# A gated product over 32 row tiles: the first tile's store as two transfers of one row each

## The chip, the cores and the metric

The kernel runs on one core of one Trainium2 chip. The metric is the device time of one execution in microseconds (us). The kernel before takes 933.05 us, the median of three runs (932.90 to 933.36).

On a core, VectorE (DVE), ScalarE (ACT) and GpSimd (POOL) compute here; SyncE (SP) only issues transfers. Transfers issued by SP stand in one queue (q1 in the profile), those issued by ACT in another (q10), and both queues are served by the same 16 DMA engines.

## The reference

The input x is 8192 x 8192 in float32. Its left half a and its right half b make the output, 8192 x 4096:

```python
def reference(x: np.ndarray) -> np.ndarray:
    a, b = np.split(x, 2, axis=-1)
    return a * (1 / (1 + np.exp(-b)))
```

So 268.4 MB are read and 134.2 MB are written, and each output element needs one sigmoid and one multiply.

## The kernel before

The 8192 rows are cut into 32 tiles of 256 rows. In a tile each of the 128 partitions holds two whole neighbouring rows (R = 2): 64 KB of input and 32 KB of output per partition, each one contiguous piece of device memory. There are two input buffers and two output buffers (SLOTS = 2), and tile i uses number i % 2 of each.

`trace` (L120) writes the order out by hand. Load 0 is put ahead of everything else (`_launch_early`, L152), then comes load 1 (L124). Then for every tile i: the work, load i+2 and store i.

- **Load** (`load`, L49): one transfer of the whole tile, 8 MB, issued by SP at L51. From load 2 on, it waits until the product of tile i-2 is done, because that work reads the buffer it overwrites.
- **Work of tiles 1 to 30** (`work_shared`, L79): ACT makes the sigmoid in place for columns 0 to 767 of both rows (L90), then for the other 3328 columns of both rows (L93). POOL multiplies the first part (L96); DVE multiplies the second (L100). POOL waits on the semaphore `ready` of the slot. That semaphore counts two things: the first sigmoid of this tile, and the landing of the store that last read this output buffer, which is store i-2. DVE waits on `both`, which counts the second sigmoid and POOL's product. DVE's product raises `product`.
- **Work of tiles 0 and 31** (`work`, L56): four pieces of half a row, 2048 columns each, with sigmoids on ACT (L64) and products on DVE (L76). The first piece's product waits on `ready` too.
- **Store of tiles 0 to 30** (`store`, L106): one transfer of 4 MB issued by ACT at L110, when the tile's last product is done. ACT works in order, so the next tile's sigmoids come behind this issue and its wait. When a store lands it adds 16 to `ready`; the planner keeps in `stored` how much the next tile in this slot has to wait for:

```python
self.to_ready[s] += 1 + self.stored[s]
self.stored[s] = 0
```

- **Store of tile 31**: four transfers of 1 MB (8 KB per partition), issued by SP as the pieces get done.

Of the kernel before, what the change touches and what calls it, by code (L numbers as in the profile page):

```python
# [13 lines left out]
class _Program:  # L14
# [105 lines left out]
    def trace(self):  # L120

        n, half = self.n_tiles, self.half
        fourths = [(slice(r, r + 1), slice(h * half // 2, (h + 1) * half // 2)) for r in range(R) for h in range(2)]
        self.load(1)  # L124
        for i in range(n):
            if i in (0, n - 1):
                self.work(i, fourths)
            else:
                self.work_shared(i)
            if i + SLOTS < n:  # L130
                self.load(i + SLOTS)
            if i < n - 1:
                self.store(i)
        for k in range(4):
            self.store(n - 1, k * half // 2, (k + 1) * half // 2, self.products - 3 + k)
# [74 lines left out]
```

## Time and profile before

| | |
|---|---|
| median of 3 runs | 933.05 us |
| the profiled execution | 933.04 us |
| its span, first to last instruction | 931.7 us |
| bytes moved, mean rate over the span | 402.67 MB, 432 GB/s |
| DVE, ACT and POOL busy | 230.6, 229.6 and 103.3 us |
| a load, issue to landing (median of 32) | 43.7 us |
| a store from ACT, issue to landing (median of 31) | 36.3 us |
| the first store, issue to landing | 33.5 us |
| ACT waits for loads at L90 | 650.0 us in 30 waits |
| POOL waits at L96, all put down to ACT's L90 | 787.3 us in 30 waits |

The page begins with the busy time of the engines, then shows the span in 40 slices. Of its DMA queues it lists packets, megabytes and the time that the packets took, as a share of 16 engines over the span. A packet is what one DMA engine moves in one piece: a row of a transfer, that is 64 KB for a load and 32 KB for a store here, or a completion of a few bytes, of which each transfer has 16. The DMA view can be asked for a stretch of time; it then counts the packets that began in that stretch. The timeline lists instructions in order: start, duration, engine, line, what is written and read, and in brackets the idle time before it and what ended it. The chain of waits is followed back from the last instruction.

### The profile page before, as it was taken

What the parts mean: (1) busy time and instruction counts of PE and PEld (TensorE: products, weight loads), DVE (VectorE), ACT (ScalarE), POOL (GpSimd) and SP (SyncE); (2) the same over time, 40 slices, a digit from 0 to 9 for tenths busy, and PEclk for the clock granted to TensorE, in tenths of its full rate; (3) what the DMA queues carried; (4) which work ended last, traced back from release to release, by engine and by line L of the source; (5) the groups of instructions that cost most, each with busy time, mean ns of one, the idle gap of its engine ahead of it and who ended that gap; (6) DMA issues with size and microseconds to landing.
All of it is one profiled execution on the core that took longest, in us unless ns stands there. A gap on an engine that the chain in (4) does not pass through costs nothing.

```text
span 931.7 us, 252 instructions
## 1 busy us (share of the span) xinstructions
DVE 230.6 (25%) x38; ACT 229.6 (25%) x69; POOL 103.3 (11%) x34
## 2 busy tenths in 40 slices
DVE  0333202332023330233302333113331133311333
ACT  1323330233311333113331133311333113332033
POOL 0011110111100111001110011110111101111010
DMA  9999999999999999999999999999999999999999
GB/s 405 428 450 428 426 452 405 450 428 428 450 422 433 428 439 439 428 428 459 439 408 430 443 454 428 412 460 411 450 428 425 453 407 449 428 428 450 425 430 405
DMA packets 9649, 402.67 MB, mean 432 GB/s; under 512 B 1072, under 2 KB 1072, under 8 KB 1072
## 3 DMA queue, kind: packets, MB, share of 16 engines
q1 hardware_dynamic: 5184, 272.63, 67.7%
q10 hardware_dynamic: 4464, 130.03, 32.3%
q14 instruction: 1, 0.01, 0.0%
HBM read 268.44 MB, written 134.22 MB: 432 GB/s over the span
## 4 chain that ended last, share of the span: by engine, by line
DMA 75%; DVE 12%; ACT 12%; DVEq 0%; issue 0%
DMA x_sb<-in_x_dram 75%; DVE o_sb L100 11%; ACT x_sb L93 9%; ACT x_sb L90 2%; DVE o_sb L76 1%; DVEq L142 0%; ACT x_sb L64 0%
## 5 line engine op out<-in xcount | busy, mean ns | idle before, releaser
L100 DVE TENSOR_TENSOR o_sb<-x_sb 128x6656 f32<-128x6656 f32 x30 | 212.8, 7092 | 654.5 <-ACT x_sb L93 654.5
L90 ACT ACTIVATE x_sb<-x_sb 128x1536 f32<-128x1536 f32 x30 | 44.5, 1482 | 650.0 <-DMA x_sb<-in_x_dram 650.0
L96 POOL TENSOR_TENSOR o_sb<-x_sb 128x1536 f32<-128x1536 f32 x30 | 103.1, 3436 | 787.3 <-ACT x_sb L90 787.3
L93 ACT ACTIVATE x_sb<-x_sb 128x6656 f32<-128x6656 f32 x30 | 172.0, 5733 | 0.0
L76 DVE TENSOR_TENSOR o_sb<-x_sb 128x2048 f32<-128x2048 f32 x8 | 17.8, 2287 | 40.4 <-ACT x_sb L64 40.4
L64 ACT ACTIVATE x_sb<-x_sb 128x2048 f32<-128x2048 f32 x8 | 14.6, 1897 | 41.0 <-DMA x_sb<-in_x_dram 41.0
L64 ACT ACT_TABLE_LOAD x1 | 1.3, 1283 | 1.4 <-PEq L176 1.4
L194 POOL MEMSET const-float32-0.0<- 128x1 f32 x1 | 0.1, 98 | 0.2 <-issue 0.2
L194 POOL MEMSET const-bfloat16-1.0<- 128x1 bf16 x1 | 0.1, 101 | 0.0
L194 POOL MEMSET const-uint8-127<- 128x1 uint8 x1 | 0.1, 101 | 0.0
L194 POOL MEMSET const-float32-1.0<- 128x1 f32 x1 | 0.1, 98 | 0.0
## 6 DMA issues: line engine op xcount, KB each, us to landing
out_dram<-o_sb ACTq DMA_DIRECT2D x31, 4096.0 KB, 36.3
out_dram<-o_sb SPq DMA_DIRECT2D x4, 1024.0 KB, 5.8
x_sb<-in_x_dram SPq DMA_DIRECT2D x32, 43.7
```

The lines of the kernel that those rows point to most:

```text
L64: sig = nc.scalar.activation(out=b, in_=b, func=mybir.ActivationFunctionType.Sigmoid)
L76: mul = nc.vector.tensor_mul(out=packed[:, r, c], in0=rows[:, r, 0, c], in1=rows[:, r, 1, c])
L90: sig = nc.scalar.activation(out=rows[:, :, 1, c0], in_=rows[:, :, 1, c0], func=sigmoid)
L93: nc.scalar.activation(out=rows[:, :, 1, c1], in_=rows[:, :, 1, c1], func=sigmoid).then_inc(self.both[s], 1)
L96: mul = nc.gpsimd.tensor_mul(out=packed[:, :, c0], in0=rows[:, :, 0, c0], in1=rows[:, :, 1, c0])
L100: mul = nc.vector.tensor_mul(out=packed[:, :, c1], in0=rows[:, :, 0, c1], in1=rows[:, :, 1, c1])
L194: nc = _bacc.Bacc("TRN2", target_bir_lowering=False, num_devices=1)
```

## The change

The first tile's store, one transfer of 128 partitions x 32 KB, becomes two transfers of 128 partitions x 16 KB. The first moves row 0 of each partition (`store(0, 0, half)`), the second row 1 (`store(0, half)`). Both are issued by ACT one behind the other, and both wait for the product of the whole tile, as the one transfer did. Each adds 16 to `ready` of slot 0 when it lands, so POOL's product of tile 2 waits for both. All other tiles are as before.

```diff
             if i + SLOTS < n:
                 self.load(i + SLOTS)
-            if i < n - 1:
+            if i == 0:
+                self.store(0, 0, half)
+                self.store(0, half)
+            elif i < n - 1:
                 self.store(i)
         for k in range(4):
             self.store(n - 1, k * half // 2, (k + 1) * half // 2, self.products - 3 + k)
```

## The prediction, made before the result was known

> **What bounds the kernel now.** I read the page first: its parts 2 to 4 say what is busy and what ended last.
>
> ```profile
> DMA  9999999999999999999999999999999999999999
> ...
> q1 hardware_dynamic: 5184, 272.63, 67.7%
> q10 hardware_dynamic: 4464, 130.03, 32.3%
> ...
> DMA 75%; DVE 12%; ACT 12%; DVEq 0%; issue 0%
> ```
>
> The two queues' packets take 67.7 + 32.3 = 100.0% of the 16 DMA engines' span, while the busiest compute engine has 25%. So the chain's 24% of DVE and ACT cannot be cut out of the time: transfers run beside them. The DMA view cut to short stretches shows how the engines divide themselves. First 4 to 33 us, loads alone; then 46 to 60.5 us, a load beside the first store; then 38.7 to 42.3 us, one round.
>
> ```profile
> DMA packets 208, 12.58 MB, mean 434 GB/s; under 512 B 16, under 2 KB 16, under 8 KB 16
> ```
>
> ```profile
> DMA packets 128, 6.29 MB, mean 434 GB/s; under 512 B 0, under 2 KB 0, under 8 KB 0
> ...
> q1 hardware_dynamic: 64, 4.19, 66.7%
> q10 hardware_dynamic: 64, 2.10, 33.5%
> ```
>
> ```profile
> q1 hardware_dynamic: 16, 1.05, 67.2%
> q10 hardware_dynamic: 16, 0.52, 33.7%
> ```
>
> Loads alone: 208 - 16 completions = 192 packets of 64 KB, 12 for each engine in 29 us, so a load row takes 29/12 = 2.417 us. Mixed: 4 packets from each queue per engine in 14.5 us, so a round is 3.625 us and a store row of 32 KB takes 1.208. The rate is 434 GB/s both ways, and **each queue gets one packet a turn, whatever its size**: equal counts, bytes 2 to 1. The timeline dates the first tiles.
>
> ```profile
> 32.82 0.38 ACTq L110 DMA_DIRECT2D out_dram<-o_sb  x1
> 44.76 1.48 ACT L90 ACTIVATE x_sb<-x_sb 128x1536 f32<-128x1536 f32 x1 [15.49 <-DMA x_sb<-in_x_dram]
> ...
> 51.91 7.09 DVE L100 TENSOR_TENSOR o_sb<-x_sb 128x6656 f32<-128x6656 f32 x1 [19.12 <-ACT x_sb L93]
> 59.03 0.36 ACTq L110 DMA_DIRECT2D out_dram<-o_sb  x1
> 73.72 1.48 ACT L90 ACTIVATE x_sb<-x_sb 128x1536 f32<-128x1536 f32 x1 [21.84 <-DMA x_sb<-in_x_dram]
> ```
>
> Tile 1 is done 14.3 us after it lands (44.76 to 59.03); tiles follow each other every 29 us, which is 8 rounds of 3.625. The end is read from the DMA view of 921.6 to 930.2 us:
>
> ```profile
> DMA packets 496, 3.67 MB, mean 427 GB/s; under 512 B 48, under 2 KB 48, under 8 KB 48
> ```
>
> The four last stores still run at full rate after the last multiply (925.5). Their 448 data packets of 8 KB are 28 per engine in 8.6 us, 0.307 each. A count of all packets gives the span: 256 load rows x 2.417 + 248 store rows x 1.208 + 32 x 0.307 = 618.7 + 299.6 + 9.8 = 928.1, plus 1.0 before the first, plus about 0.7 for the first and 0.8 for one slow load row as the first store joins (16 packets at 34 to 38.7 us took 69.1% of 4.7 us, 3.25 each): 930.6 of 931.7 us. Nothing but packets is in it.
>
> **The change part by part.** Only the first store changes. *Bytes and packets*: 8 rows of 32 KB per engine become 16 of 16 KB. No 16 KB row is in the trace; from below it is half a 32 KB row, 0.604, from above two 8 KB rows, 0.614. Sixteen cost 9.66 to 9.82 against 8 x 1.208 = 9.66: **+0.0 to +0.2 us**, and I take 0.604, as the rate is 434 from 32 KB up and 427 at 8 KB. A gain is excluded, since no stretch passes 434. One more completion is 0.01 us.
>
> *Issue*: a second DMA on ACT right behind the first, its wait already met, 0.38 us by the first's row. Behind it is tile 1's sigmoid, not due before 43.5, so it costs nothing; without that cover it would cost 0.38.
>
> *Turns*: a store row is half as big, so beside a load the round is 2.417 + 0.604 = 3.021, not 3.625: **loads go faster, the first store slower**. I check the count on the kernel before. Store packets start at 38.7 (in 34 to 38.7 only q1 has any). A completion counts as a turn: store 0's 8 rows lie between 7 load rows and load 1's completion, 38.7 + 8 x 1.208 + 7 x 2.417 = 65.3, and it lands at 66.3 (32.82 + 33.5 of the DMA view), 1.0 later. Load 2: 9 load rows (the last of load 1, eight own) and 10 store rows, 38.7 + 21.75 + 12.08 = 72.5; tile 2 starts at 73.72, 1.2 later. Now with halves:
>
> - Load 1 lands after one load row and two halves: 38.7 + 2.42 + 1.21 + 1.2 = 43.5, 1.2 earlier; tile 1 is done at 57.8.
> - Load 2: 38.7 + 21.75 + 10 x 0.604 + 1.2 = 67.7, 6.0 earlier.
> - Store 0: 16 halves and the first half's completion are 17 turns against 15 load rows and two completions: 38.7 + 9.66 + 36.26 = 84.6, landing at 85.6 instead of 66.3.
>
> *A new wait*: tile 2 writes the buffer that store 0 reads, and POOL's multiply (L96) waits for it. Its sigmoid is there at 69.2, the store at 85.6, so **POOL waits 16 us**, ends at 89.1, and DVE (L100) runs from 89.2 to 96.3. Without the wait DVE would have ended at 82.0; before, it was 88.0. Behind DVE's product hang load 4 on SP and store 2 on ACT, and behind store 2 on ACT tile 3's sigmoids. Does the DMA run dry? At 84.6 load 3 has 2 rows left: 84.6 + 2 x 2.417 + 2 x 1.208 = 91.9, and then the load queue is empty. Store 1, issued at 57.8, has 6 rows left, alone: 7.25 us, to 99.1. Load 4 and store 2 are issued at 96.3. From issue to first packet I have the first of the last stores: issued at 918.94, and packets of its queue begin at 920.9, 2.0 us. So they are ready at 98.3, **0.8 us before the engines run dry**. What hides the whole stall is this backlog of store 1; each microsecond beyond 0.8 is paid in full. A load that joins may cost one slow row as at 35 us, +0.8, or nothing as when the last stores joined; I take nothing, the nearer in kind (a queue used before).
>
> *Afterwards*: load 4 has 8 load rows and 7 store rows, 99.1 + 19.3 + 8.5 + 1.2 = 128.1, where before it was 131.7, so a lead of 3.6 us stays. Store 1 lands at 102.6, POOL of tile 3 waits for it, DVE ends at 113.3; load 5 is in the queue well before 127. Store 2 lands at 131.6, tile 4's POOL ends at 135.1, and its second sigmoid at 135.2: the wait is covered. Then each tile repeats in 29 us, 3.6 us early. At the end the last load lands 3.6 earlier, at 911.1, but that much more of the stores is still to move: the bytes are the same, the engines never idle, and the last packet comes when it did. **Sum: +0.0**, between +0.0 and +1.0 (packets 0.2, slow row 0.8).
>
> The profiled execution took 933.04 us, 1.3 more than its span, and the median is 933.05, so the forecast is 933.04 + 0.06 = **933.1 us**.
>
> **The rivals.**
> - *The shares do not move* (a turn is a fixed amount of bytes, not a packet), and the change shows nothing of the above: 933.0. Against it: a completion of 4 bytes takes a turn in the counts above. 10%.
> - *The engines run dry* (slower): tile 2's stall outlasts store 1's backlog at 99.1 us. It decides from 2.8 us between issue and first packet. For it: the first store was issued at 32.8 and its packets began at 38.7, 5.9 us. Then load 4 and store 2 begin at 102.2, 3.1 us late, all of it lost: 936.1. Against it: that was ACT's first transfer, behind load rows of 2.4 us each; and the last stores needed 2.0. 10%.
> - *The second transfer's start is not overlapped*: 2.0 us from issue to first packet as idle engines, 935.1. Against it: the three later last stores follow one another at 427 GB/s. 3%. The Trainium skill's page "DMA: Bandwidth & Descriptors", section "Anatomy of one DMA — SWDGE (gpsimd) path", puts a fixed cost of about 2.0 us on every DMA beside its bytes, and would add that much here; the 427 GB/s over the end of this trace speaks against adding it up.
> - *The end follows the last load* (faster): the chain of waits goes back from the last multiply to loads, and these come 3.6 us early: 929.4. Against it: after the last multiply 5 us of packets are left at full rate. 3%.
>
> **How the numbers follow.** My forecast has 74%. About 0.2% (1.9 us) is what a measurement here can tell from no change. Forecast and unmoved shares are within it: same 84%; dry engines and start cost: slower 13%; faster 3%. Range: below, the slow row of 35 us could vanish, 933.1 - 0.8 = 932.3; above, the sum's +1.0 and the start cost's 935.1. So 932.3 to 935.1, leaving out the rest of the dry case and the faster case, some 12%.
>
> **What would show it.** The DMA view at 46 to 57 us should have equal packet counts and bytes 4 to 1. Tile 1's first sigmoid should start at 43.5, tile 2's at 67.7, with POOL's wait of 16 us put down to the store; DVE of tile 2 should end at 96.3; load 4 should land at 128.1, the later ones 3.6 us early; and no stretch between 85 and 105 us should be below 420 GB/s. I am wrong if tile 2 is done after 97.1 or a load issued into an empty queue needs more than 2.8 us.

## The result, and the profile after

| | before | changed |
|---|---|---|
| median of 22 runs each | 933.26 us | 936.57 us |
| lowest and highest | 932.90 to 934.14 | 932.93 to 963.15 |
| the profiled execution, its span | 933.04, 931.7 | 938.78, 937.5 |

The changed kernel is slower by 0.3%: the ratio is 1.0029 with an interval of 1.0016 to 1.0042. The two longest of its runs, 951.99 and 963.15 us, count as slow runs and are left out of the ratio, though their granted clock is 1.0 like that of the others. The forecast was 933.1 us, 932.3 to 935.1, so it was wrong.

The kernel before is steady; the changed one is not. Of its 22 runs 7 took 932.9 to 933.6 us, the forecast's time; 9 took 936.3 to 937.2, 4 took 938.0 to 942.2, and 2 took 952 and 963. So the question is what differs from run to run.

The page of the changed kernel, with the same lines as the page of before:

```profile
DMA  9999999999999999999999999999999999999997
...
q1 hardware_dynamic: 5184, 272.63, 67.4%
q10 hardware_dynamic: 4608, 130.03, 32.2%
...
DMA 75%; DVE 12%; ACT 11%; POOL 0%; DVEq 0%; issue 0%
```

Only the last digit of the DMA row has changed, from 9 to 7, and the two queues sum to 99.6% of a longer span. So the engines are as full as before until the very end. The store queue has 144 packets more: 128 more rows, because 128 rows of 32 KB became 256 of 16 KB, and 16 completions more.

The timeline of the changed kernel follows the forecast for the first 98 us. Columns: start, duration, engine and line, then the idle time before and what ended it.

```profile
43.27 1.48 ACT L90 ACTIVATE x_sb<-x_sb 128x1536 f32<-128x1536 f32 x1 [13.97 <-DMA x_sb<-in_x_dram]
...
57.55 0.36 ACTq L110 DMA_DIRECT2D out_dram<-o_sb  x1
67.47 1.48 ACT L90 ACTIVATE x_sb<-x_sb 128x1536 f32<-128x1536 f32 x1 [17.08 <-DMA x_sb<-in_x_dram]
...
85.57 3.42 POOL L96 TENSOR_TENSOR o_sb<-x_sb 128x1536 f32<-128x1536 f32 x1 [37.30 <-DMA out_dram<-o_sb]
89.02 7.09 DVE L100 TENSOR_TENSOR o_sb<-x_sb 128x6656 f32<-128x6656 f32 x1 [31.50 <-POOL o_sb L96]
96.14 0.36 ACTq L110 DMA_DIRECT2D out_dram<-o_sb  x1
...
113.14 0.36 ACTq L110 DMA_DIRECT2D out_dram<-o_sb  x1
...
129.10 1.48 ACT L90 ACTIVATE x_sb<-x_sb 128x1536 f32<-128x1536 f32 x1 [25.43 <-DMA x_sb<-in_x_dram]
```

Tile 1 lands at 43.27 (forecast 43.5), tile 2 at 67.47 (67.7). POOL's product of tile 2 starts at 85.57 (85.6); its sigmoid was there at 67.47 + 1.48 = 68.95, so it waited 16.6 us for the store. Load 4 and store 2 are issued at 96.14 (96.3). The large stall is there, as foreseen. In the list of waits, POOL's wait for a store now stands first, with 25 of its 30 tiles; this one is the longest:

```profile
POOL o_sb L96 <- DMA out_dram<-o_sb: 643.7, 25, 37.3
```

The 37.3 us are all of POOL's idle time before it, of which 16.6 us lie behind the sigmoid.

From 129 us on the forecast and the trace part. The last load should have landed at 911.1, 3.6 us earlier than before (914.68); it landed later:

```profile
916.79 7.31 ACT L64 ACTIVATE x_sb<-x_sb 128x2048 f32<-128x2048 f32 x4 [22.36 <-DMA x_sb<-in_x_dram]
```

The stretches at the end tell how. The last two columns are the share of time in which the 16 DMA engines moved packets, and GB/s. First the changed kernel, then the kernel before:

```profile
926.00:932.00 6.00, 1.63 (x1) 0.00 (x0) 0.00 (x0) 1.00 0.99 412
932.00:937.40 5.40, 0.00 (x0) 0.00 (x0) 0.00 (x0) 1.00 0.09 38
```

```profile
926.00:931.70 5.70, 0.00 (x0) 0.00 (x0) 0.00 (x0) 1.00 0.84 356
```

Up to 932 us the engines are full. From there on the share is 0.09, and 0.09 x 16 is 1.4 engines: one or two of the sixteen still work, for 5 us, while the others are done. The packets of each engine can be followed, since each begins where the one before on its engine ends. Fourteen engines end between 931.9 and 932.4 us, one at 934.7, one at 937.1. Before, all sixteen ended between 930.7 and 931.4. **Two engines of sixteen are late, and the transfer is done when the last engine is.**

They are not late from the start. Every load ends with one completion on each engine; this table, worked out from the packet records of the changed kernel, has for some loads the median time of the sixteen, the deviation of the two latest, and that of the other fourteen:

```
load's completion     the two engines      the other fourteen
128.4 us              -0.88   -0.88        -0.11 to 0.33
476.4                  0.47    1.75        -0.15 to 0.28
650.7                  1.90    2.52        -0.18 to 0.24
766.7                  2.07    3.13        -0.27 to 0.40
882.8                  2.18    4.17        -0.29 to 0.58
```

They begin 0.88 us ahead and slip by 3.1 and 5.1 us over 26 tiles. (In the first row the two stand apart as the earliest; between 130 and 420 us they pass through the others and can't be told from them by time alone.)

What sets these two apart happened when load 4 joined. The packets of the two kinds of engine there (S and L a row of a store and of a load, s a completion of store 1, each with its start):

```
fourteen engines: S 98.06   s 99.27   L 99.28    S 101.69   L 102.90
two engines:      S 98.50   L 99.70   s 102.12   L 102.12   S 104.54
```

The DMA view of the changed kernel in two short stretches shows it in counts of packets and MB. From 99.2 to 99.8 us:

```profile
DMA packets 30, 1.05 MB, mean 1748 GB/s; under 512 B 14, under 2 KB 14, under 8 KB 14
...
q1 hardware_dynamic: 16, 1.05, 403.9%
```

and from 102.11 to 102.14 us:

```profile
DMA packets 4, 0.13 MB, mean 4369 GB/s; under 512 B 2, under 2 KB 2, under 8 KB 2
...
q1 hardware_dynamic: 2, 0.13, 1007.5%
```

In the first stretch all sixteen begin load 4's first row, but only 14 small packets, store 1's completions, go with them. The two missing ones come 2.4 us later, each with a second load row right behind. On fourteen engines the store's completion comes **ahead of row 0** of the load, on two it comes **behind row 0**. Since every queue then goes on by turns, an engine keeps that order, tile after tile, to the end.

### The profile page after: what moved, and what is told of

Its sections match the earlier page's. It is cut to its first block, busy times and chain, and to the rows that moved or that the text cites. A ratio compares the mean times of both kernels' runs of the same rounds, so it can differ in the third digit from the quotient of the medians.

```text
span 937.5 us, 253 instructions
## 1 busy us (share of the span) xinstructions
DVE 230.6 (25%) x38; ACT 229.6 (24%) x69; POOL 103.2 (11%) x34
## 4 chain that ended last, share of the span: by engine, by line
DMA 75%; DVE 12%; ACT 11%; POOL 0%; DVEq 0%; issue 0%
DMA x_sb<-in_x_dram 70%; DVE o_sb L100 11%; ACT x_sb L93 8%; DMA out_dram<-o_sb 5%; ACT x_sb L90 2%; DVE o_sb L76 1%; POOL o_sb L96 0%; DVEq L145 0%; ACT x_sb L64 0%
```

## The experiments

Seventeen kernels were run, one of them twice. Their expectations speak of theories by letters. A, B and C are rivals from the start: A is the order of turns at the moment when load 4 joins, B the stall and POOL's wait for stores, C a fixed cost of a second transfer; e1 has them in full. G (the compute engines slow the load rows) and H (the order of loads and stores does so alone) are in full at e13. The other letters are explained where they come up.

For reading the runs it helps to have their common measure first. In the profile of each run the packets of every engine were followed from 100 to 880 us, and noted, for every load on every engine: behind which of its eight rows a store's completion comes, and how much longer than 8 x 2.418 us its rows took. "Ahead" means ahead of row 0.

```
kernel                 completion behind   loads x engines   extra us per load
before                 row 5               418               0.001
changed                ahead / row 0       339 / 52          0.001 / 0.170
e1_late                ahead               368               0.116
e2_early               ahead / row 0       335 / 26          0.001 / 0.202
e5_early_again         row 0 / ahead       250 / 144         0.662 / 0.759
e16_after_dve          row 1 / row 0       250 / 128         0.005 / 0.301
e3_parts               row 6               386               0.001
e9_first_half          row 5               357               0.001
e4_tiny1               row 4 / row 5       234 / 147         0.001 / 0.000
e6_dry_split           row 4 / row 5       246 / 124         0.000 / 0.004
e7_dry_clean           row 4 / row 5       254 / 145         0.001 / 0.000
e8_one                 row 5 / row 4       412 / 18          0.001 / 0.006
e18_shift_less         row 5               406               0.001
e10_shift              row 0               404               0.603
e11_shift_one          row 0 / row 7       368 / 20          0.547 / 0.504
e12_shift_eight        row 0 / row 7       241 / 130         0.560 / 0.126
e13_shift_nowork       row 0               397               0.563
e14_shift_dve          row 0 / row 1       361 / 28          0.589 / 0.445
e15_shift_noact        row 0               396               0.586
```

All lines but the first two are of runs told below; e17 turned out to be e10 again and has no line. Entries of fewer than 18 loads are left out. Wherever completions come behind row 0 for load after load, the loads are slow; with them behind rows 4 to 6 they are slow in none of these runs. Behind other rows, or ahead, they are free in some runs, and slow in e5, e11, e12 and e14, where more than half of the engines stand behind row 0, and in e1.

### The halves by themselves

**Only the first half is stored.** Row 1 of each partition of tile 0 is left out of the output.

```diff
-            if i < n - 1:
+            if i == 0:
+                self.store(0, 0, half)
+            elif i < n - 1:
                 self.store(i)
```

> The kernel before, but of the first store only the first transfer of the change is made: row 0 of each partition, 8 packets of 16 KB per engine. Row 1 of the first tile (half its output) is left out, so 2.1 MB less are written: 8 x 0.604 = 4.8 us less for each engine. Eight packets are eight turns, as many as the whole store has in the kernel before, so that tile 2 does not wait, the load queue does not run empty and the loads are not ahead. Theory A: 928.0 to 929.5 in nearly every run, with no slow rows. Rival D (half rows of 16 KB themselves cost, or put the engines out of step): above 930.

Measured: 928.19 us, median of 5 runs, ratio 0.9952 (0.9938 to 0.9965). The 2.1 MB left out are 8 rows of 16 KB per engine, 8 x 0.604 = 4.8 us, and 933.26 - 4.8 = 928.4. So rows of 16 KB move at their price. There is only one transfer here, so this says nothing of the start of a second one.

**Two transfers cut by partitions instead of by rows**, in the kernel before:

```diff
-            if i < n - 1:
+            if i == 0:
+                self.store(0, parts=slice(0, 64))
+                self.store(0, parts=slice(64, P))
+            elif i < n - 1:
                 self.store(i)
```

> The first store goes as two transfers, but each of 64 partitions with whole 32 KB rows, not of half rows. Each engine then has the 8 packets of 32 KB of the kernel before and one completion more. Theory A: store 0 lands at most one load row (2.4 us) later, tile 2 does not wait for it, the load queue never runs empty, all engines stay in step: 933.0 to 933.6. Theory B: no stall, 933.0 to 933.6. Theory C (fixed cost of a second transfer): 935 to 936.5.

Measured: 937.19 us, median of 5, ratio 1.0034 (1.0021 to 1.0047). The kernel before had 934.04 us beside it, so this is outside what any of the three theories gave. It was no clean control, since it has a loss of its own and at once: between 54 and 68 us, in the second of the two transfers, most rows of 32 KB took 1.3 to 1.8 us instead of 1.21, and after 75 us no row is slow. In the first of the two most rows took 1.21 us, and some 1.3 to 1.44. The Trainium skill's page "SBUF — State Buffer", section "Door 1: The DMA port swizzle (why `[64,N]` ≈ `[32,N]`)", says that 64 partitions in a row reach no more ports than 32 do; the second transfer's rows fit that and most of the first's do not, and no run here counts ports. The change of this study keeps all 128 partitions and has no such rows.

### The moment at which load 4 joins

Tile 2's product may be moved a little by shifting columns between POOL and DVE in tile 2 alone.

**Later** (the changed kernel and one line):

```diff
-        c0, c1 = slice(0, FIRST), slice(FIRST, self.half)
+        first = 960 if i == 2 else FIRST
+        c0, c1 = slice(0, first), slice(first, self.half)
```

> The halved store stays; in tile 2 alone POOL takes 960 instead of 768 columns of each row, so that tile 2 is done about 0.45 us later and load 4 comes into its empty queue about 0.45 us later (POOL +0.86, DVE -0.41 us by the rows of the profile). Theory A (the loss comes from load 4 becoming ready just as the engines end the last row of store 1, so that two engines take their turns in another order than the other fourteen, fall out of step and slip until they are a round of 3.6 us behind): the instant is moved off the engines' boundary (98.06 to 98.50 us in the profile after), all engines take the same order, load 31 lands near 911.5 us, and the time is 933.0 to 933.8, in nearly every run. Theory B (the stall of tile 2 and POOL's wait for stores in every tile cost the time): the stall is 0.45 us longer, so 936.5 to 937.2. Theory C (a fixed cost of the second transfer): 936.5, unchanged.

Measured: 933.24 us, median of 12 runs: 8 of them 933.09 to 933.28, then 934.11, 935.86, 938.67 and 941.42. Ratio to the kernel before 1.0009 (0.9992 to 1.0025). Tile 2 is done at 96.91 instead of 96.14. The profiled run is one of the long ones, but in it the restart is clean; the DMA view of 99.2 to 100.2 us of this kernel has all sixteen completions beside the sixteen first rows:

```profile
DMA packets 32, 1.05 MB, mean 1049 GB/s; under 512 B 16, under 2 KB 16, under 8 KB 16
...
q1 hardware_dynamic: 16, 1.05, 246.8%
```

Its loss came otherwise: one engine fell 2.7 us behind between 127 and 156 us and stayed there, and from about 800 us on rows on all engines were slow (0.7 to 1.1 us a load). So a store cut in two, with the whole stall (tile 2 done 0.8 us *later* than in the changed kernel), costs nothing in most runs, and a second transfer's start neither. Theory B asked for 936.5 to 937.2 us here, theory C for 936.5. The cause of the longer runs is not found.

**Earlier**, `first = 416`, twice the same kernel:

> The halved store stays; in tile 2 alone POOL takes 416 instead of 768 columns of each row, so that tile 2 is done about 0.8 us earlier (POOL -1.57, DVE +0.75 us). Theory A (turn order at the boundary of store 1's last row): load 4 becomes ready between two boundaries of the engines, all take the same order, 933.0 to 933.8 in nearly every run. Theory B (stall): 0.8 us less of it, 935.5 to 936.5. Theory C (fixed cost of the second transfer): 936.5, unchanged.

> The same kernel as e2_early, for another trace: four of its six times lay at 959 to 962 us and one at 939.5, and the trace at hand is of a short one. Theory A as it stands (an engine out of step slips by one round, 3.6 us) does not give 26 us. If it is a lasting loss of rate, the trace has rows that take longer in every stretch from about 100 us on, some 3% (26 of 830 us), with no idle DMA; if it is one stall, one stretch of 25 us has a low rate and the rest is at 434 GB/s.

Measured: 939.52, 959.31, 959.01, 961.82, 960.32 and 961.06 us as e2, 957.2 as e5. All three theories had expected less, A among them, which took the new moment for a safe one. Tile 2 is done at 95.57, only 0.57 us earlier than in the changed kernel, and the time is mostly 20 us longer: no price of a stall or a transfer in these expectations gives that. The profile of the 939.52 run has one engine behind row 0; over the tiles it slips until it is 4.7 us late (0.202 us a load), and ends at 937.8 where the others end at 932.7. The DMA view of the 957.2 run from 99.2 to 100 us:

```profile
DMA packets 22, 1.05 MB, mean 1311 GB/s; under 512 B 6, under 2 KB 6, under 8 KB 6
...
q1 hardware_dynamic: 16, 1.05, 302.9%
```

Sixteen first rows, six completions; ten engines have the load first. In the 939.52 run of the same kernel it was one engine, so the moment itself is not the same in every run. And its page:

```profile
q1 hardware_dynamic: 5184, 272.63, 68.1%
q10 hardware_dynamic: 4608, 130.03, 31.5%
```

The share of q1 times the span is the time in which engines moved load packets: 0.681 x 955.9 = 651.0 us, against 0.677 x 931.7 = 630.8 before. The same bytes took 20.2 us more. The stores took 0.315 x 955.9 = 301.1, as before (0.323 x 931.7 = 300.9). So all of it is in load rows, and in this run the six other engines, with the completion ahead, are slow as well.

**Earlier by another way**: in the changed kernel the first multiply of each tile goes from POOL to DVE.

```diff
-        mul = nc.gpsimd.tensor_mul(out=packed[:, :, c0], in0=rows[:, :, 0, c0], in1=rows[:, :, 1, c0])
+        mul = nc.vector.tensor_mul(out=packed[:, :, c0], in0=rows[:, :, 0, c0], in1=rows[:, :, 1, c0])
```

> The changed kernel (halved first store) with POOL's multiply given to DVE in all tiles; nothing is left out. Theory G with POOL as the cause: 933.0 to 934 in nearly every run, where the changed kernel has 936.6. Theory G with ACT, or theory H: 935 or above in about half of the runs, as in the changed kernel.

Measured: 947.73 us, median of 940.11, 944.02, 951.45 and 952.27; ratio 1.0154 (1.0089 to 1.022). Tile 2 is done at 94.39, 1.75 us earlier than in the changed kernel, and load 4 joins in two groups of engines. Its DMA view of 98.0 to 98.6 us, then of 99.2 to 99.8:

```profile
q1 hardware_dynamic: 11, 0.72, 277.1%
q10 hardware_dynamic: 5, 0.16, 63.2%
```

```profile
q1 hardware_dynamic: 5, 0.33, 125.9%
```

At 98.3 us eleven engines begin the load while five begin the last store row, and these five begin the load after it. Eleven then have the completion behind row 1, five behind row 0. In this one run the two orders stand side by side, beside the same work: the eleven lose 0.005 us a load, the five 0.301. Deviation of the completions from the median, as in the table above:

```
load's completion   the five engines                  the other eleven
184.1 us            2.11  2.21  2.23  2.24   2.38     -0.20 to 0.18
416.1               3.16  3.27  3.48  4.10   5.79     -0.20 to 0.18
648.2               4.22  5.11  6.53  6.87   8.42     -0.30 to 0.65
880.2               6.91  7.63  9.37  9.88  11.87     -0.30 to 0.65
```

The span is 942.7, 11.0 us over that of before. The latest engine alone slipped by 9.5 us between the first and the last line of this table.

### Running dry, and being out of step, by themselves

Four kernels take the kernel before and disturb it in the middle.

**The load queue runs empty.** Load 12 is held back, so that it joins a running store as load 4 does in the change:

```diff
+        if i == 12:
+            ins = self.nc.sync.dma_start(out=self.xs[s][:, :], in_=self.x[i]).then_inc(self.loaded[s], 16)
+            ins._wait_ge(self.ready[1], self.to_ready[1] + 1 + self.stored[1])
+            return ins
```

> The kernel before with its whole first store; load 12 alone waits for the first sigmoid of tile 11 instead of the product of tile 10, so that the load queue is empty for some 5 us while store 10 still has rows. No store is halved and nothing else waits. By the latencies of the profile after, load 12 becomes ready 5.03 us after load 11's last row, inside the spread (4.85 to 5.52 us) of the engines' boundaries between two rows of store 10. Theory A (a load queue that starts again beside running store rows splits the engines' order): several runs at 936 or above, as in the changed kernel. Theory B (it is the stall of POOL and of tile 2, or the halved rows): 933.1 to 934.2 like the kernel before.

Measured: 934.96 us, median of 11 (934.06 to 935.52), ratio 1.0011 (1.0003 to 1.002). The engines split, 12 behind row 0 and 4 behind row 1, but for this one load only; two loads later all but one stood behind row 4 and stayed there. In that one load no row was slow. The time lies between the two that were expected.

The second one moves the moment by `first = 560 if i == 11 else FIRST` as well:

> As e6_dry_split, but tile 11's first sigmoid has 560 instead of 768 columns of each row, so that load 12 is ready 0.35 us earlier, 4.68 us after load 11's last row, between two boundaries (4.31 and 4.85 us). Theory A with the boundary as the cause: all engines take the same order, most runs at 933.1 to 934.2. If this kernel is as slow as e6_dry_split, the restart itself costs, wherever it falls. Theory B: 933.1 to 934.2 for both.

Measured: 934.26 us, median of 11 (933.89 to 935.67), ratio 1.0008 (0.9999 to 1.0017). Here fifteen engines stood behind row 1 for that load, and then behind row 4. Against the kernel before beside them (933.85 us) the two medians are 1.1 and 0.4 us longer, and the second is within the noise. Behind row 0 for one load was no loss here. In e10, told below, the first load in that order already took 0.2 to 0.4 us longer on fifteen engines, so the order at that place is not the whole condition.

**A small transfer** behind load 10 on SP's queue, first one of 256 bytes from device memory to device memory, which came as 16 pieces on all engines, then one of 4 bytes that only one engine gets:

```diff
+            if i == 8:
+                self.tiny(1)
```

> The kernel before, with its whole first store, and one small extra transfer on SP's queue right behind load 10: 256 bytes of x into a scratch tensor, one packet on one DMA engine. That engine alone has one turn more and falls out of step with the other fifteen; nothing stalls. Theory A: the engine slips until it is a round behind, loads land later by up to 3.6 us at the end: 935.5 to 937. Theory B (stall): 933.1 to 933.4. Theory C (fixed cost per transfer, if not hidden): about 935 to 936, and the same for an extra transfer that uses all sixteen engines, which is tried next.

Measured: 936.11 us, median of 10 (935.41 to 936.55), ratio 1.0023 (1.0014 to 1.0032). The store rows beside it were some 1.5 us longer once, around 307 us, and hardly a row after that. It moved all engines, so it says nothing of one, and that its time lies in theory A's range is luck.

> The kernel before, with one extra transfer of 4 bytes from x into SBUF on SP's queue behind load 10, one packet on one DMA engine only. (The extra transfer of e4_tiny1 had spread over all sixteen engines, sixteen bytes each, written to device memory, so that it was no test of one engine.) That engine alone has one or two turns more than the others. Theory A (one engine out of step slips until it is a round behind): load 31 lands up to 3.6 us later and the time is 935.5 to 937. If an engine out of step keeps its distance and loses nothing, load 31 lands as before and the time is 933.1 to 934.2, and theory A needs something more than the order.

Measured: 933.82 us, median of 11 (933.53 to 934.16), ratio 1.0002 (0.9993 to 1.0011). One engine is 1.3 us out of step with the others for 550 us, behind row 4 where they are behind row 5, and loses nothing. Being out of step alone is not the cause.

### The order built into the kernel before

If the order behind row 0 costs, a kernel without halves, without a stall and without an empty queue must be slow in it. Here the whole first store is issued by ACT only behind the first sigmoid of tile 1:

```diff
         sig.then_inc(self.ready[s], 1)
+        if i == 1:
+            self.store(0)
...
-            if i < n - 1:
+            if 0 < i < n - 1:
                 self.store(i)
```

> The kernel before with its whole first store, issued on ACT behind the first sigmoid of tile 1 instead of ahead of it, some 10 us later. Loads run alone for these 10 us and get ahead of the stores, as in the changed kernel, but tile 2 hardly waits (to about 75 us) and the load queue never runs empty, so that no queue starts again. Theory A: all engines stay in step, 933.0 to 934.2. Rival E (a longer backlog of stores behind the loads costs by itself, since POOL waits for a store in every tile): 936 or above.

Measured: 953.0 us, median of 4 (952.43 to 953.82), ratio 1.0213 (1.0199 to 1.0227). That all sixteen engines would stand behind row 0 was not foreseen: the expectation was 933 us by theory A, since all would be in step, and the time fell to the side of rival E. The trace shows what it is. The store is issued at 41.54 instead of 32.8 us, and all sixteen engines have the completion behind row 0. Its page, where q1 takes 0.681 x 951.9 = 648.2 us, 17.5 more than before, and q10 0.316 x 951.9 = 300.8, the same:

```profile
q1 hardware_dynamic: 5184, 272.63, 68.1%
q10 hardware_dynamic: 4464, 130.03, 31.6%
```

The slow rows are rows 1 and 2 of each load. Mean extra time by row of a load, 0 to 7:

```
e10_shift       .022 .242 .283 .041 .005 .001 .000 .001
e5_early_again  .106 .341 .232 .017 .002 .007 .007 .003
```

So the loss is in the load rows themselves and not in a wait, which speaks against rival E. In e16, too, DVE waits for a store in 29 tiles, and the eleven engines behind row 1 lose nothing. Those eleven took load 4's first row a store row earlier than the five, so that in that run a greater lead of the loads by itself didn't cost either. The loss is the one of e5, without the change. It is so all through the run; the same stretch of 29 us of this kernel, and then of the kernel before:

```profile
600.00:629.00 29.00, 7.09 (x1) 7.12 (x2) 3.43 (x1) 1.00 0.99 420
```

```profile
600.00:629.00 29.00, 7.09 (x1) 7.14 (x3) 3.45 (x2) 1.00 1.00 434
```

The engines are as full (0.99, 1.00), and move less. A full queue is not a full rate: only GB/s, not the share, shows the loss.

Two kernels add the small transfer to this one, for one engine and for eight, to move them out of the order:

> e10_shift with the extra transfer of 4 bytes of e8_one behind load 10, one packet on one DMA engine, which puts that engine 1.3 us out of step. In the kernel before (e8_one) an engine out of step lost nothing. Theory F (out of step costs only where loads run ahead of the stores, because then other rows meet): slow rows on that engine in each tile, it slips until it is a round of 3.6 us behind, 935.5 to 937. If being out of step is harmless here too: 933.0 to 934.2, and what slows the rows in the changed kernel stays open.

> e10_shift with an extra transfer of 8 rows of 8 bytes behind load 10, one packet on each of eight DMA engines, which puts eight of the sixteen out of step with the other eight, as the split of ten and six did in the trace of 957 us. Theory F: slow rows in every tile from about 330 us on, 3% of the remaining 600 us, 945 to 955. If it is harmless: 933.0 to 934.2.

Measured: 952.94 us (949.01 to 953.46), ratio 1.0202 (1.0185 to 1.0219); and 952.44 us (951.94 to 953.36), ratio 1.0207 (1.0193 to 1.0221); 4 runs each. The end does not move, since the engines that stay behind row 0 set it. In the second eight engines did move, to row 7, and lost 0.126 us a load against 0.560; in the first the one engine that moved lost 0.504, nearly as much as the rest. So it isn't an engine's own order alone when most others stand behind row 0.

Is it the compute engines, which touch the same memory? In the next kernel tiles 2 to 30 compute only 32 columns per operation, and most of the output is left out; the one after moves POOL's multiply to DVE (the diff shown for the changed kernel above); the third cuts the second sigmoid to 64 columns, so that the gate of the other columns is left out.

```diff
+        if i > 1:
+            c0, c1 = slice(0, 32), slice(FIRST, FIRST + 32)
```

```diff
-        nc.scalar.activation(out=rows[:, :, 1, c1], in_=rows[:, :, 1, c1], func=sigmoid).then_inc(self.both[s], 1)
+        c2 = slice(FIRST, FIRST + 64)
+        nc.scalar.activation(out=rows[:, :, 1, c2], in_=rows[:, :, 1, c2], func=sigmoid).then_inc(self.both[s], 1)
```

> e10_shift (whole first store, issued late, 953 us) with almost no compute: in tiles 2 to 30 each sigmoid and each multiply takes 32 columns of each row instead of 768 or 3328, so that nearly all of their output is left out; all transfers are as in e10_shift. The traces so far have their slow load rows (rows 1 to 3 of a load) nearly all while ACT and POOL work, and an engine has them when it takes its rows 0 and 1 back to back. Theory G (the load rows meet the compute engines' work, which a pair of load rows in a row makes visible): 932 to 935, no slow rows. Theory H (the rows slow each other by the order of loads and stores alone, and the compute only happens at the same time): 950 to 954, the same slow rows.

> e10_shift with POOL's multiply of columns 0 to 767 given to DVE in all tiles (DVE 8.7 us a tile instead of 7.1, POOL idle); nothing is left out. Mean excess of a load row in e10_shift: 0.30 us beside POOL and ACT, 0.17 beside ACT alone, 0.02 beside DVE. Theory G with POOL as the cause: 933 to 940. Theory G with ACT as the cause: 945 to 953. Theory H: 950 to 954.

> e10_shift with ACT's second sigmoid cut to 64 of its 3328 columns in each row (the rest of that sigmoid is left out, so most of the output lacks it); POOL and DVE as before. Theory G with ACT as the cause: 933 to 940. Theory G with POOL as the cause: 948 to 953. Theory H: 950 to 954.

Measured, 4 runs each: 952.55 us, ratio 1.0204 (1.0188 to 1.0219); 952.66, 1.0205 (1.019 to 1.022); 952.52, 1.0204 (1.0189 to 1.0219). Three equal times. The stretch of the first of them, with 0.23, 0.40 and 0.32 us of compute where there were 7.09, 7.12 and 3.43:

```profile
600.00:629.00 29.00, 0.23 (x1) 0.40 (x2) 0.32 (x1) 1.00 1.01 426
```

Compute has no part in it that these runs show. The Trainium skill's page "SBUF — State Buffer", section "SBUF: two separate sides", says that compute and DMA reach that memory through ports of their own; these three times agree.

### Two that moved nothing

**The first store behind both sigmoids** of tile 1 (e10 with two lines exchanged), meant to put the completion behind another row:

```diff
-        if i == 1:
-            self.store(0)
         nc.scalar.activation(out=rows[:, :, 1, c1], in_=rows[:, :, 1, c1], func=sigmoid).then_inc(self.both[s], 1)
+        if i == 1:
+            self.store(0)
```

> As e10_shift, but the whole first store is issued behind both sigmoids of tile 1, some 5.7 us later still. The loads get some 2.4 rows further ahead, so that each store ends about two rows later in a load: its completion then stands behind row 2 or 3 of a load instead of behind row 0, so that two load rows come back to back there. If it is the position behind row 0 that slows the next rows (the kernel before has it behind row 5 and loses nothing): 933 to 936. If every lead of the loads costs: 953 or above.

Measured: 952.88 us, median of 4 (952.6 to 953.09), ratio 1.0207 (1.0192 to 1.0222). The timeline of this kernel shows why it is e10 again:

```profile
41.14 1.48 ACT L90 ACTIVATE x_sb<-x_sb 128x1536 f32<-128x1536 f32 x1 [12.02 <-DMA x_sb<-in_x_dram]
41.15 0.38 ACTq L112 DMA_DIRECT2D out_dram<-o_sb  x1
42.53 5.73 ACT L93 ACTIVATE x_sb<-x_sb 128x6656 f32<-128x6656 f32 x1
```

The issue stands behind two sigmoids in the program, and goes out 0.01 us after the first has *begun*.

**A pause on ACT** ahead of the first store of the kernel before (a sigmoid of 2700 columns that nobody needs, written to the free output buffer):

```diff
+            if i == 0:
+                pause = self.nc.scalar.activation(out=self.os[1][:, :2700], in_=self.os[0][:, :2700], func=mybir.ActivationFunctionType.Sigmoid)
+                pause._wait_ge(self.product, self.done[0])
```

> As e10_shift, but the first store is issued only about 2.4 us later than in the kernel before: ACT first does one sigmoid of 2700 columns, from the first tile's output into the still unused second output buffer, which tile 1 overwrites. The loads get about one row ahead, and a store's completion stands behind row 6 of a load instead of row 5. If only the position behind row 0 costs: 932.9 to 934.2. If the cost grows with the lead of the loads: 935 to 942.

Measured: 933.32 us, median of 10 (933.01 to 933.86), ratio 0.9999 (0.999 to 1.0009). The completion stayed behind row 5, so it tells nothing of the rows between.

## Why the prediction was wrong, point by point

**Right: what bounds the kernel, the turns and the bytes.** A 16 KB row does take a turn of its own. The DMA view of the changed kernel from 46 to 57 us, which was to show bytes 4 to 1:

```profile
q1 hardware_dynamic: 64, 4.19, 87.9%
q10 hardware_dynamic: 48, 0.79, 16.7%
```

64 rows of 64 KB and 48 of 16 KB: 4 to 1 for each packet. The counts differ only by the edges of the stretch, which holds the start of the load row four times and that of the store row three times. All dates up to 98 us came to within 0.25 us, for this reason.

**Right: the stall and its cover.** POOL's wait, the end of DVE's product and the new issue came as forecast, and the engines did not idle: in the packet records no engine has a gap over 0.05 us between 85 and 105 us. The forecast's own test, no stretch below 420 GB/s there, would have misled: the stretch of 85 to 105 us shows 406, but its count takes whole packets by their start, and one load row on each engine more or less is 16 x 65.5 KB in 20 us, 52 GB/s. The other sign, a load that needs more than 2.8 us into an empty queue, misled too: load 4 was issued at 96.14 and its first row began at 99.27, 3.1 us later, but until then the engines moved store 1's last rows.

**Right: the second transfer's start costs nothing** (e1, which has both halves: 8 runs of 12 at 933.1 to 933.3), and the shares do move. The Trainium skill's page "DMA: Bandwidth & Descriptors", section "Anatomy of one DMA — SWDGE (gpsimd) path", which the prediction sets beside this rival, gives its 2.0 us for transfers that GpSimd issues; those here are issued by ACT and SP. The rivals of the dry engines and of the added start both gave a time near the one measured (936.1 and 935.1 against 936.57), and both for a reason that the trace excludes. A time that fits is no proof of its mechanism.

**Wrong: the Sum.** It said: "the bytes are the same, the engines never idle, and the last packet comes when it did", between +0.0 and +1.0. The bytes were the same and the engines did not idle, but the last packet came 5.7 us later (937.1 against 931.4). The step failed in two places.

- *A row has no fixed price.* The working gave a load row 2.417 us wherever it stands. Where the store's completions come behind row 0 of every load, rows 1 and 2 take longer: 0.17 to 0.30 us a load with one to five engines in that order, 0.55 to 0.66 with eight or more. Over 29 loads that is 0.603 x 29 = 17.5 us for e10, as much as its load packets grew as far as the rounded shares tell. In the changed kernel, from load 4 on, the load rows of its two engines took 3.5 and 5.9 us longer in all. Less the 0.88 us by which both were ahead at first, that is 2.6 and 5.0: their tails, 934.7 and 937.1 less 932.2, are 2.5 and 4.9.
- *Sixteen engines are not one.* Their turns begin and end up to 0.44 us apart (98.06 and 98.50 in the trace). The forecast had load 4 ready at 98.3, "0.8 us before the engines run dry", and used this only as a margin against idling. By the trace it lay among the sixteen turns, and so decided the order on each engine for the rest of the run. Being earlier by 0.57 us (e2, e5) made the time 940 to 962; being later by 0.77 (e1) made it 933.1 to 933.3 in 8 runs of 12. With the margin read as idling, later should have been worse.

Also a little off: load 4 landed at 129.10 instead of 128.1, as eight store rows went ahead of its completion and not seven (99.28 + 8 x 2.418 + 8 x 1.21 = 128.3, and its completions are at 128.4). And the fourteen undisturbed engines ended 1.0 us later than before, at the upper bound of the sum.

**What is shown and what is not.** Shown: the order at load 4's joining differs between engines and runs; the engines behind row 0 are the ones that lose (e16, e2 and the changed kernel, within one run each); a kernel without the change loses 20 us when all its engines have that order (e10); halves, an empty queue, one engine out of step and compute don't cost this. Not shown: why rows 1 and 2 are slow in that order, and why twelve engines had it for one load of e6 without loss (which addresses loads and stores touch at the same time shifts with the order too, and was not varied by itself); why in the run of 957 us the six engines with the completion ahead were slow too, and in e11 the one behind row 7, when most others stood behind row 0; what slowed the few long runs of e1; and, as only one run of the changed kernel has a trace, that its usual 936.3 to 937.2 us is one engine or two behind row 0. That is likely, as these give 3 to 5 us in the runs with a trace, but it was argued. The chip of each of the changed kernel's 22 runs isn't on record, so a part of their spread may go with the chip; e2 spread from 939.5 to 961.8 us on one chip. Completions behind row 2 or 7 on all engines were not tried. No kernel that was run is faster than the kernel before with all its output.

## What to carry to other kernels

When transfers bound a kernel, a full DMA row in the page doesn't mean that it runs at its full rate: compare GB/s in a stretch in the middle, and look at the end for a stretch with one or two engines left. A change at the start of such a kernel may set the order in which the queues take turns for all that follows, so keep a restart away from the moment at which the engines' turns end, and ask for a spread of many runs, not one, as the sign of an order left to chance. Move the edge both ways by a few tenths of a microsecond; if earlier is worse, it isn't a stall. A clean restart isn't all of it: e10 has no restart and is slow, and a few runs of e1 have a clean one and are long.

## What the runs showed of the hardware that was not expected

- The order of turns on an engine lasts: set at 99 us, it was the same at 880 us, and one engine 1.3 us out of step kept so for 550 us (e8).
- A load row of 64 KB took 2.418 us in nearly all places, but 0.23 to 0.34 more on average as rows 1 and 2 of a load in the runs in which the other queue's completion came behind row 0 on most engines (e10, e5).
- Of two stores from 64 partitions each, one behind the other, the second moved most of its 32 KB rows in 1.3 to 1.8 us, not 1.21 (e3).
- ACT sent out a transfer 0.01 us after the start of the first of two sigmoids that stand ahead of it (e17), 7.1 us before the second ended.
- A transfer of 256 bytes was cut into 16 pieces, one for each engine, and cost about 2 us (936.11 against 934.04 beside it), where one of 4 bytes on one engine cost nothing that shows (933.82 against 933.85) (e4, e8).
